# Second group's first two v products moved ahead of the first group's other five

## The chip, the cores and the metric

The kernel runs on one core of one Trainium2 chip. The metric is the device time of one execution in microseconds (us). Before the change three runs took 3236.82, 3237.32 and 3232.02 us, median 3236.82.

## The reference, cut to what matters

Two layers of a bidirectional encoder on 1024 tokens with 1024 features. The first layer mixes tokens by latent attention, the second by dilated windows in three groups; each ends with an MLP. The change touches the v part of the second layer's input projection, three products of 1024 x 1024 by 1024 x 1024, one for each group:

```python
h = rms_norm(x, norm_mix[i]) * (1 + scale1) + shift1
...
def dilated_mixer(h, pos, w_in, g_q, g_k, rel_bias, w_o):
    proj = (h @ w_in).reshape(B, S, N_DIL_GROUPS, 3, DIL_HEADS, DIL_HEAD_DIM)
    for gi, (window, dilation) in enumerate(DIL_GROUPS):
        ...
        v = proj[:, :, gi, 2]
```

shift1 and scale1, like the gates and the MLP's shift and scale, come from the conditioning vector c by `ada_w`, the modulation.

## The kernel before

Activations and weights are float32. Each matrix is split into a high part that fp32r holds (ScalarE, ACT, copies it: L121) and a low part (VectorE, DVE, subtracts: L122), and every matmul becomes three, high by high, high by low, low by high (`mm3`, L425 to L427).

`dil_v` (L1597 to L1776) computes v for each group as a 2 x 2 block product with seven multiplications in place of eight. h and the weights are cut into quarters of 512 x 512. The products of a group, by index i, are L11 R11, L12 R21, S2 T2, S1 T1, S3 T3, L22 T4 and S4 R22. The L and S sides come from h: L11 and L12 are halves for the first 512 tokens, whose high and low parts (hT) the MLP before left ready; L22 and S1 to S4 need the other 512 tokens as well. The R and T sides come from the weights: `sums` makes T1 = 12 - 11, T3 = 22 - 12, T2 = 22 - T1 and T4 = T2 - 21 in place, in the tiles (wvr) that held the quarters. Each product is 4 token tiles x 4 steps of 128 features x 3 = 48 matmuls of 128 x 128 by 128 x 512 into four PSUM banks (psv).

The loop over the 21 products (L1713 to L1774, n counts them) does for each: evict the product before (L1646), issue loads of weight quarters (L431, two DMAs of 512 KB each on the queue of SyncE, SP), make the weight sums, split the weight for the next product (`form`, wvh and wvl), split one of the h sides, and issue the 48 matmuls. Beside the first product the other 512 tokens are normalised (xh), transposed by PE (pst) and modulated (hk, half by ACT, half by DVE); beside the second their sums s1, s3 and S2, S4 are made on DVE (`h_sums`), and S2 is split (hsh, hsl). So S2 T2, the third product, is the first that needs them. Products 4 to 17 (counted from 0) also carry two `ada_step` each: one step loads 512 KB of modulation weights (adaw, L262) and adds them up on DVE (adacc: L175 the first of a vector, L176 the others).

Evictions: i = 0 copies the banks to vp by ACT; on DVE, i = 2, 3 and 4 add into vp, and i = 1, 4, 5 and 6 make vz, which POOL's queue stores. The weight tiles, the splits and vp come from one pool of 29 tiles of 4 KB a partition ("gran"); a load waits until its tile's last reader is through. A scheduler puts the instructions of each engine in order; what `pinned` marks keeps the order of the program.

Of the kernel before, what the change touches and what calls it, by code (L numbers as in the profile page):

```python
# [41 lines left out]
class K:  # L42
# [1045 lines left out]
    def mlp7(self, l, early, R, steps, xd, out, more=(), nxt=None, keep=None):  # L1088
# [16 lines left out]
        with self.tc.tile_pool(name="psM", bufs=8, space=PSUM, reuse_waits="tile") as psp:  # L1105
# [81 lines left out]
            def d_form(i, g, ld):  # L1187
                rn = order2[i][1]
                u, q = ld
                r = []  # L1190

                def split(x):
                    r.extend(self.X("d" + k, (P, 2, 512)) for k in "hl")
                    self.split(*r[-2:], x)

                split(u)
                if rn == "R11":
                    split(q["11"])
                    tt(q["12"], q["12"], q["11"], ALU.subtract)
                    kept[("T1", g)], kept[("T3", g)] = q["12"], q["11"]  # L1200
                elif rn == "T2":
                    kept[(rn, g)] = w = self.G("w2T", (P, 2, 512), F32)
                    tt(w, q["22"], kept[("T1", g)], ALU.subtract)
                    split(w)
                    tt(kept[("T3", g)], w, kept[("T3", g)], ALU.subtract)
                elif rn == "T4":
                    w = self.X("w2s", (P, 2, 512), F32)
                    tt(w, q["21"], kept[("T2", g)], ALU.subtract)
                    split(w)
                else:  # L1210
                    split(q[rn[1:]] if rn[0] == "R" else kept[(rn, g)])
                return r
# [14 lines left out]
            seq = [(c, i) for c in range(E) for i in (0, 2)]  # L1227
# [65 lines left out]
            quad = lambda n: [self.G(n, (P, 2, 512), F32) for _ in range(2)]  # L1293
            at = lambda q, t: q[t // 2][:, t % 2, :]
            xs = [None] * 8
            last = len(dsteps) - 1
            c1, c2 = slice(0, 512), slice(512, 1024)
            V, done = {}, []
# [29 lines left out]
            for n, (i, gr) in enumerate(dsteps):  # L1328
# [10 lines left out]
                if i in (3, 5) and gr < 4:  # L1339
                    t = i * 2 - 6 + gr  # L1340
                    xs[t] = self.load(xd[t * P : (t + 1) * P, :], (P, 1024), "x")
                if (i, gr) == (3, 4):
                    g = self.gate(l, 1)
# [253 lines left out]
    def dil_v(self, xs, mods, at0, keep, w11, f11, vd):  # L1597
# [5 lines left out]
        sub = lambda o, x, y: self.pinned(tt(o, x, y, ALU.subtract))  # L1603

        prod = [("L11", "R11"), ("L12", "R21"), ("S2", "T2"), ("S1", "T1"), ("S3", "T3"), ("L22", "T4"), ("S4", "R22")]
        seq = [(g, i) for g in range(3) for i in range(7)]
        hd = self.dp.tile([2, P, 2, 512], F32, name="h21")
        h0 = at0.tiles
        L = {f"L1{j + 1}": [[h0[k][2 * j + p] for k in range(2)] for p in range(2)] for j in range(2)}
        W = {(0, "11"): w11}  # L1610
        F = {0: f11}
        V = {}
        Hh, at1 = self.h_at()

        def load(g, q):
            W[(g, q)] = self.dil_w(g, q)

        def form(n):
            g, i = seq[n]
            F[n] = self.w_form(W[(g, ("11", "21", "T2", "T1", "T3", "T4", "22")[i])])  # L1620
            if i == 6:
                del W[(g, "22")]

        def sums(g, i):

            for k in range(2):
                w = lambda q: W[(g, q)][k]
                if i == 0:
                    sub(w("11"), w("12"), w("11"))
                elif i == 1:  # L1630
                    sub(w("12"), w("22"), w("12"))
                    sub(w("22"), w("22"), w("T1"))
                else:
                    sub(w("21"), w("T2"), w("21"))
            for old, new in {0: (("11", "T1"),), 1: (("12", "T3"), ("22", "T2")), 2: (("21", "T4"),)}[i]:
                W[(g, new)] = W.pop((g, old))

        quad = lambda n: [self.G(n, (P, 2, 512), F32) for _ in range(2)]
        el = lambda q, t: q[t // 2][:, t % 2, :]

        def out(g, t, c, o, ps, op=ALU.add):
            z = self.T("vz")
            tt(z, o, ps, op)
            nc.gpsimd.dma_start(out=vd[g][t * P : (t + 1) * P, c * 512 : (c + 1) * 512], in_=z)

        def evict(n, pss):  # L1646
            g, i = seq[n]
            if i in (0, 3):
                V["PQ"[i // 3]] = quad("vp")
            for t, ps in enumerate(pss):  # L1650
                p, q = (el(V[x], t) if x in V else None for x in "PQ")
                if i == 0:
                    nc.scalar.activation(p, ps, AF.Copy)
                elif i == 1:
                    out(g, t, 0, p, ps)
                elif i == 2:
                    tt(p, p, ps)
                elif i == 3:
                    tt(q, p, ps)
                elif i == 4:  # L1660
                    tt(p, p, ps)
                    out(g, t + 4, 1, q, ps)
                elif i == 5:
                    out(g, t + 4, 0, p, ps, ALU.subtract)
                else:
                    out(g, t, 1, q, ps)
            if i > 4:
                del V["PQ"[i - 5]]


        A, S = {}, {}
# [1 line left out]
        def h_form(name, src, alloc):  # L1673
            L[name] = []
            for x in src:
                f = [alloc("hs" + k, (P, 2, 512)) for k in "hl"]
                self.split(*f, x)
                L[name].append(f)
            if name == "L22":
                for k in range(2):  # L1680
                    Hh[k][2:4] = [f[k] for f in L[name]]
# [15 lines left out]
        def h_sums(k):  # L1697
            S.setdefault("S1", []).append(self.X("s1", (P, 2, 512), F32))
            S.setdefault("S3", []).append(self.X("s3", (P, 2, 512), F32))
            a11, a12, a21, a22 = keep[k], keep[2 + k], A[0][k], A[1][k]  # L1700
            tt(S["S1"][k], a21, a22)
            tt(S["S3"][k], a11, a21, ALU.subtract)
            tt(a11, S["S1"][k], a11, ALU.subtract)
            tt(a12, a12, a11, ALU.subtract)
            nc.gpsimd.dma_start(out=hd[k], in_=a21)

        with self.tc.tile_pool(name="psV", bufs=8, space=PSUM, reuse_waits="tile") as psp:
            done = None
            load(0, "21")
            load(0, "12")  # L1710
            xh = self.xhat(xs, self.X, pinv=True)
            last = len(seq) - 1
            for n, (g, i) in enumerate(seq):  # L1713
                if done:
                    evict(*done)
                if i == 0:
                    load(g, "22")
                elif i == 5:
                    load(g, "22")
                    if g < 2:  # L1720
                        load(g + 1, "11")
                elif i == 6 and g < 2:
                    load(g + 1, "21")
                    load(g + 1, "12")
                if i < 3:
                    sums(g, i)
                if n < last:
                    form(n + 1)
                if n == 1:
                    for k in range(2):  # L1730
                        h_sums(k)
                    for x, k in (("S2", 0), ("S4", 2)):
                        S[x] = keep[k : k + 2]
                    h_form("S2", S.pop("S2"), self.X)
                elif 1 < n < 6:
                    x = ("S1", "S3", "L22", "S4")[n - 2]
                    h_form(x, A.pop(1) if x == "L22" else S.pop(x), self.G if x == "L22" else self.X)
                ps = [psp.tile([P, 512], F32, tag="m", name=self.nm("psv")) for _ in range(4)]
                l, f = L[prod[i][0]], F.pop(n)
                for d in range(4):  # L1740
                    if n == 0 and d in (2, 3):
                        h_chunks(xh, 2 * d - 4, psp)
                    for t in range(4):
                        ts = slice(t * P, (t + 1) * P)
                        (lh, ll), (rh, rl) = ([x[:, d % 2] for x in y[d // 2]] for y in (l, f))
                        self.mm3(ps[t], lh[:, ts], ll[:, ts], rh, rl, d == 0, d == 3)
                done = n, ps
                if 3 < n < last - 2:
                    for _ in range(2):
                        self.ada_step(psp, "m")  # L1750
                if n == 0:
                    keep, xh = list(keep), None
                if n == last - 2:
                    raws = [self.load(hd[k], (P, 2, 512), "h21r", alloc=self.X) for k in range(2)]
                    w = self.dil_weights(0, 0, self.X)
                elif n == last - 1:
                    for raw in raws:
                        f = [self.G("hT" + k, (P, 2, 512)) for k in "hl"]
                        self.split(*f, raw)
                        for k in range(2):  # L1760
                            Hh[k].insert(len(Hh[k]) - 2, f[k])
                    raws = None
                    w = w()
            evict(*done)
        return at1, w

# [636 lines left out]
```

## Time and profile before

| | us |
|---|---|
| median of three runs (lowest, highest) | 3236.82 (3232.02, 3237.32) |
| the profiled execution's own time | 3228.74 |
| its span, first to last instruction | 3227.0 |
| busy in the span: DVE, ACT, POOL | 2383.3, 1733.2, 919.4 |
| mean granted clock of TensorE | 0.990 |
| psv matmuls, first to last start | 1421.6 to 1669.7 |
| evictions vz, vp by DVE; vp by ACT, each | 0.686, 0.687; 0.599 |

Times in rows of the profile count from the first instruction. PE is the matmul engine, PEld its weight loads. The stage of the v products is 248 us of 3227.

### The profile page before, as it was taken

The numbers are of one execution on the slowest core, as the hardware profiler recorded it, in microseconds if no ns is written. First come the engines' busy times: TensorE is split into PE (matmuls) and PEld (weight loads), VectorE is DVE, ScalarE is ACT, GpSimd is POOL, SyncE is SP. The second block draws the span as 40 slices with busy tenths as digits, with TensorE's granted clock in tenths as the row PEclk, the third lists the DMA queues.
The fourth block names the chain that finished last, engine by engine and source line by source line (L and its number), as shares of the span: only waits on it lengthen the run. The fifth ranks groups of instructions, "written<-read, shape, count | busy, mean of one in ns | idle before, by whom it ended". The sixth has DMA issues, their size and how long they took to land. (4 is left out here: it accounts for less than half of the span.)

```text
span 3227.0 us, 50801 instructions
## 1 busy us (share of the span) xinstructions
PE 3127.3 (97%) x18034; PEld 2645.7 (82%) x18034; DVE 2383.3 (74%) x4243; ACT 1733.2 (54%) x3507; POOL 919.4 (28%) x1226
## 2 busy tenths in 40 slices
PE   6999999999999999989999999999999999999999
PEld 6877677778788788877889999998998888887887
DVE  6677777746987776588757778777888588778566
ACT  5547777754554433543226677667665264444332
POOL 7464556530111100000123445444454001110010
PEclk9999999999999999999999999999999999999999
DMA  5352322253555779544638877888778536448554
GB/s 193 121 190 80 108 84 92 70 167 111 177 200 175 268 220 307 179 148 162 224 125 187 184 179 178 191 190 174 173 165 202 167 106 214 150 152 311 204 190 129
DMA packets 538926, 552.31 MB, mean 171 GB/s; under 512 B 199429, under 2 KB 421042, under 8 KB 538666
## 3 DMA queue, kind: packets, MB, share of 16 engines
q1 hardware_dynamic: 500874, 443.00, 48.4%
q0 software_dynamic: 27360, 91.31, 7.6%
q10 hardware_dynamic: 10432, 14.68, 1.6%
q8 instruction: 144, 2.36, 0.3%
q14 instruction: 116, 0.95, 0.1%
HBM read 376.17 MB, written 132.62 MB: 158 GB/s over the span
## 5 line engine op out<-in xcount | busy, mean ns | idle before, releaser
L426 PE MATMUL psm<-dl,dh 128*128 128x512 f32 x896 | 350.7, 391 | 8.3 <-DVE dl L122 8.2
L425 PE MATMUL psm<-hf,wf 128*128 128x512 f32 x896 | 350.4, 391 | 2.6 <-ACT wf L121 2.6
L426 PE MATMUL psm<-hf,wf 128*128 128x512 f32 x896 | 349.7, 390 | 0.0
L427 PE MATMUL psm<-dh,dl 128*128 128x512 f32 x896 | 349.7, 390 | 0.0
L427 PE MATMUL psm<-hf,wf 128*128 128x512 f32 x896 | 347.2, 390 | 0.4 <-DVE wf L122 0.4
L425 PE MATMUL psm<-dh,dh 128*128 128x512 f32 x896 | 335.9, 392 | 5.2 <-ACT dh L121 5.2
L425 PE MATMUL psproj<-wqkh,hTp 128*128 128x256 f32 x1024 | 302.0, 295 | 0.0
L427 PE MATMUL psproj<-wqkh,hTp 128*128 128x256 f32 x1024 | 290.4, 284 | 0.0
L426 PE MATMUL psproj<-wqkl,hTp 128*128 128x256 f32 x1024 | 290.3, 283 | 0.0
L121 ACT ACTIVATE dh<-ufr 128x1024 fp32r<-128x1024 f32 x112 | 118.3, 1056 | 175.3 <-PE psm L427 50.0
L426 PEld LDWEIGHTS psm<-dl,dh 128*128 128x128 f32 x896 | 168.7, 188 | 46.5 <-DVE dl L122 11.6
L425 PEld LDWEIGHTS psproj<-wqkh,hTp 128*128 128x128 f32 x1024 | 196.6, 192 | 8.5 <-issue 0.4
L425 PEld LDWEIGHTS psm<-dh,dh 128*128 128x128 f32 x896 | 168.5, 189 | 42.7 <-ACT dh L121 7.8
L425 PEld LDWEIGHTS psm<-hf,wf 128*128 128x128 f32 x896 | 168.7, 188 | 40.1 <-ACT wf L121 5.5
L427 PEld LDWEIGHTS psm<-hf,wf 128*128 128x128 f32 x896 | 168.5, 188 | 35.8 <-DVE wf L122 1.2
L426 PEld LDWEIGHTS psm<-hf,wf 128*128 128x128 f32 x896 | 168.7, 188 | 35.0
L427 PEld LDWEIGHTS psm<-dh,dl 128*128 128x128 f32 x896 | 168.8, 188 | 34.6
L426 PEld LDWEIGHTS psproj<-wqkl,hTp 128*128 128x128 f32 x1024 | 196.8, 192 | 0.2 <-DVE wqkl L122 0.2
L427 PEld LDWEIGHTS psproj<-wqkh,hTp 128*128 128x128 f32 x1024 | 196.4, 192 | 0.2
L122 DVE TENSOR_TENSOR dl<-ufr,dh 128x1024 fp32r<-128x1024 f32 x112 | 136.9, 1222 | 77.3 <-ACT dh L121 58.6
L756 DVE TENSOR_REDUCE mx<-pmx 128x1 f32<-128x512 f32 x256 | 165.1, 682 | 29.5 <-PE pmx L754 29.3
L122 POOL TENSOR_TENSOR pl<-p,ph 128x1024 fp32r<-128x1024 f32 x58 | 141.3, 2436 | 138.8 <-ACT ph L121 133.8
(400 smaller groups left out, 8926.4 us busy)
## 6 DMA issues: line engine op xcount, KB each, us to landing
ufr<-uf SPq DMA_DIRECT2D x112, 512.0 KB
adaw<-in_ada_w SPq DMA_DIRECT2D x96, 512.0 KB
w2r<-in_mlp_w SPq DMA_DIRECT2D x96, 512.0 KB
w1r<-in_mlp_w SPq DMA_DIRECT2D x64, 512.0 KB
bt<-bias SPq DMA_DIRECT2D x128, 256.0 KB
wqkr<-in_dil_w_in SPq DMA_DIRECT2D x96, 256.0 KB
qkv<-st SPq DMA_DIRECT2D x32, 512.0 KB
hraw<-qkv SPq DMA_DIRECT2D x32, 512.0 KB
```

What stands on the lines that cost most here:

```text
L121: nc.scalar.activation(hi, src, AF.Copy)
L122: (lo_eng or nc.vector).tensor_tensor(lo, src, hi.bitcast(F32), op=ALU.subtract)
L425: mm(out, lh, rh, start=first, stop=False)
L426: mm(out, lh, rl, start=False, stop=False)
L427: mm(out, ll, rh, start=False, stop=last)
L756: nc.vector.tensor_reduce(maxes[h][:, 2 * j + b : 2 * j + b + 1], ps, op=ALU.max, axis=AX.X)
```

## The change

The order of the 21 products becomes: the first group's first two, the second group's first two, then the first group's other five, the second group's other five, and the third group's seven. The second group's quarters 11 and 21 are loaded early for these two products, dropped, and loaded again for the sums; that is four DMAs of 512 KB more. The first group's sums and the splits of S1, S3, L22 and S4 move two products later, the second group's first sums stand beside the first group's last product. The modulation steps begin two products earlier (n = 2), and products 7 and 8, the last of the first group, have none. A group's eviction tiles are kept by group. In the MLP one condition is written twice.

```diff
@@ mlp7, d_form
                 if rn == "R11":
                     split(q["11"])
+                if rn == "R11":
                     tt(q["12"], q["12"], q["11"], ALU.subtract)
@@ dil_v
-        seq = [(g, i) for g in range(3) for i in range(7)]
+        seq = [(0, 0), (0, 1), (1, 0), (1, 1)] + [(g, i) for g in range(3) for i in range(7) if g == 2 or i > 1]
...
             if i == 6:
                 del W[(g, "22")]
+            if g == 1 and i < 2:
+                del W[(g, ("11", "21")[i])]
...
-                V["PQ"[i // 3]] = quad("vp")
+                V[g, "PQ"[i // 3]] = quad("vp")
...
-                if i == 0:
+                if n == 0:
+                    load(1, "11")
+                if (g, i) == (0, 1):
+                    load(1, "21")
+                if i == 0 and g != 1:
                     load(g, "22")
+                elif i == 4 and g == 0:
+                    load(1, "11")
+                    load(1, "12")
                 elif i == 5:
                     load(g, "22")
-                    if g < 2:
-                        load(g + 1, "11")
+                    if g == 0:
+                        load(1, "22")
+                    elif g == 1:
+                        load(2, "11")
                 elif i == 6 and g < 2:
                     load(g + 1, "21")
-                    load(g + 1, "12")
-                if i < 3:
+                    if g:
+                        load(2, "12")
+                if (g, i) == (0, 6):
+                    sums(1, 0)
+                    sums(1, 1)
+                if n in (2, 3):
+                    sums(0, n - 2)
+                elif i == 2 or i < 2 and g == 2:
                     sums(g, i)
...
-                elif 1 < n < 6:
-                    x = ("S1", "S3", "L22", "S4")[n - 2]
+                elif 3 < n < 8:
+                    x = ("S1", "S3", "L22", "S4")[n - 4]
...
-                if 3 < n < last - 2:
+                if 1 < n < last - 2 and n not in (7, 8):
                     for _ in range(2):
                         self.ada_step(psp, "m")
```

Lines behind the edits move by up to 18 (the vz and wvr sums stand at L1602 before and at L1603 after). Engine by engine, the programs hold the same rows in the same order ahead of the first product and behind the twelfth; POOL's rows are the same throughout.

The first place is PE at the start of the third product. Before, in a piece of its rows (operation, bank written <- weights moved through, h side held):

```order
L427 MATMUL psv_19266<-wvh_19115,hT_3880_18987 128x512
L425 MATMUL psv_19345<-wvh_19233,hsh_19255 128x512
L425 MATMUL psv_19346<-wvh_19233,hsh_19255 128x512
L425 MATMUL psv_19347<-wvh_19233,hsh_19255 128x512
L425 MATMUL psv_19348<-wvh_19233,hsh_19255 128x512
L426 MATMUL psv_19345<-wvl_19234,hsh_19255 128x512
L426 MATMUL psv_19346<-wvl_19234,hsh_19255 128x512
L426 MATMUL psv_19347<-wvl_19234,hsh_19255 128x512
L426 MATMUL psv_19348<-wvl_19234,hsh_19255 128x512
L425 MATMUL psv_19417<-wvh_19329,hsh_19337 128x512
```

And after the change, PE at the same place:

```order
L427 MATMUL psv_19268<-wvh_19117,hT_3880_18987 128x512
L425 MATMUL psv_19339<-wvh_19235,hT_3811_18667 128x512
L425 MATMUL psv_19340<-wvh_19235,hT_3811_18667 128x512
L425 MATMUL psv_19341<-wvh_19235,hT_3811_18667 128x512
L425 MATMUL psv_19342<-wvh_19235,hT_3811_18667 128x512
L426 MATMUL psv_19339<-wvl_19236,hT_3811_18667 128x512
L427 MATMUL psv_19339<-wvh_19235,hT_3812_18668 128x512
L426 MATMUL psv_19340<-wvl_19236,hT_3811_18667 128x512
```

The third product now reads hT, which is there since the MLP, in place of S2's hsh; four matmuls with the high part stand ahead of the first that needs the low part wvl. In each later half of a product four matmuls with wvh stand so ahead of wvl, in some places with four of the next product.

The second place is DVE ahead of that low part. Before, from the h sums to the third product's first wvl (vz evicts the second product, wvr are the weight sums):

```order
L1602 TENSOR_TENSOR s_3931_19249<-hk_18784,hk_19185 128x1024
L1602 TENSOR_TENSOR vz_19315<-vp_19223,psv_19263 128x512
L1602 TENSOR_TENSOR wvr_19105<-wvr_19105,wvr_18812 128x1024
L1602 TENSOR_TENSOR wvr_19082<-wvr_19107,wvr_19082 128x1024
L1602 TENSOR_TENSOR hk_18669<-s_3928_19241,hk_18669 128x1024
L1602 TENSOR_TENSOR hk_18784<-s_3930_19248,hk_18784 128x1024
L1602 TENSOR_TENSOR vz_19318<-vp_19223,psv_19264 128x512
L1602 TENSOR_TENSOR vz_19321<-vp_19224,psv_19265 128x512
L122 TENSOR_TENSOR wvl_19234<-wvr_19105,wvh_19233 128x1024
```

And DVE after the change, to the same product's first wvl; the modulation of the second chunk's first hk stands just ahead of this piece:

```order
L1603 TENSOR_TENSOR s_3932_19243<-hk_19149,hk_19162 128x1024
L1603 TENSOR_TENSOR s_3933_19244<-hk_18669,hk_19149 128x1024
L1698 TENSOR_SCALAR hk_19200<-pst_19207,mod_17521,mod_17903 128x512
L1603 TENSOR_TENSOR hk_18669<-s_3932_19243,hk_18669 128x1024
L1603 TENSOR_TENSOR s_3934_19250<-hk_19187,hk_19200 128x1024
L1603 TENSOR_TENSOR s_3935_19251<-hk_18784,hk_19187 128x1024
L1603 TENSOR_TENSOR hk_18893<-hk_18893,hk_18669 128x1024
L122 TENSOR_TENSOR hsl_19258<-hk_18669,hsh_19257 128x1024
L1603 TENSOR_TENSOR hk_18784<-s_3934_19250,hk_18784 128x1024
L1603 TENSOR_TENSOR vz_19317<-vp_19225,psv_19265 128x512
L1603 TENSOR_TENSOR vz_19320<-vp_19225,psv_19266 128x512
L122 TENSOR_TENSOR wvl_19236<-wvr_19105,wvh_19235 128x1024
```

The weight sums of the first group left this piece; the h sums and S2's low part stand in it ahead of wvl.

The third place is DVE in the fifth product, S2 T2 after the change, from its first low part (wvl_19408) to its second:

```order
L122 TENSOR_TENSOR wvl_19408<-wvr_19109,wvh_19407 128x1024
L1603 TENSOR_TENSOR wvr_19111<-wvr_19111,wvr_18814 128x1024
L122 TENSOR_TENSOR hsl_19578<-s_3935_19251,hsh_19577 128x1024
L1603 TENSOR_TENSOR vz_19473<-vp_19397,psv_19415 128x512
L176 SCALAR_TENSOR_TENSOR adacc_19395<-adaw_19470,cond,adacc_19395 128x1024
L1603 TENSOR_TENSOR vz_19476<-vp_19397,psv_19416 128x512
L1603 TENSOR_TENSOR vz_19479<-vp_19398,psv_19417 128x512
L1603 TENSOR_TENSOR vz_19482<-vp_19398,psv_19418 128x512
L1603 TENSOR_TENSOR wvr_19076<-wvr_19109,wvr_19076 128x1024
L1603 TENSOR_TENSOR wvr_19078<-wvr_19111,wvr_19078 128x1024
L122 TENSOR_TENSOR wvl_19412<-wvr_19111,wvh_19411 128x1024
```

Four adacc now stand on DVE ahead of wvl_19412. Before, none stood there until the low parts of the third and the fourth product were made.

More of the change, by code (lines that the diff above doesn't have):

```diff
@@ L1648, in evict @@
             if i in (0, 3):
-                V["PQ"[i // 3]] = quad("vp")
+                V[g, "PQ"[i // 3]] = quad("vp")
             for t, ps in enumerate(pss):
-                p, q = (el(V[x], t) if x in V else None for x in "PQ")
+                p, q = (el(V[g, x], t) if (g, x) in V else None for x in "PQ")
                 if i == 0:
@@ L1667, in evict @@
             if i > 4:
-                del V["PQ"[i - 5]]
+                del V[g, "PQ"[i - 5]]
         A, S = {}, {}
```

## The prediction

> **What bounds the kernel now.** I read the shares by engine first, then the stretches of this stage, then who waited for whom, then single rows. In the page's first part, each entry is an engine's busy time and instructions:
>
> ```profile
> PE 3127.3 (97%) x18034; PEld 2645.7 (82%) x18034; DVE 2383.3 (74%) x4243; ACT 1733.2 (54%) x3507; POOL 919.4 (28%) x1226
> ```
>
> TensorE (PE) is busy for 97% of the span, so only idle or slow PE time can be won. The busy times by stretch, for 60 us of the stage of the v products (start and end, length, then PE, PEld, DVE, ACT, POOL busy, granted clock, DMA share, GB/s):
>
> ```profile
> 1433.00:1445.00 12.00, 12.00 (x69) 10.44 (x68) 12.00 (x14) 3.06 (x5) 1.26 (x3) 1.00 0.38 134
> 1445.00:1457.00 12.00, 6.45 (x21) 4.13 (x20) 12.00 (x13) 10.02 (x11) 1.99 (x4) 0.75 0.38 130
> 1457.00:1469.00 12.00, 11.62 (x43) 9.06 (x41) 12.00 (x12) 4.98 (x5) 0.00 (x0) 0.82 0.00 0
> 1469.00:1481.00 12.00, 12.00 (x54) 9.95 (x53) 11.33 (x15) 3.19 (x3) 0.00 (x0) 1.00 0.20 52
> 1481.00:1493.00 12.00, 12.00 (x54) 9.95 (x53) 9.62 (x13) 2.12 (x2) 1.08 (x2) 1.00 0.76 260
> ```
>
> PE is full except from 1445 to 1469, where it also gets a granted clock of 0.75 and 0.82. DVE is full from 1433 until then: VectorE bounds this piece. The waits of PE from 1421 to 1670, the whole stage, are few:
>
> ```profile
> PE psv L425 <- ACT wvh L121: 2.4, 1, 2.4
> PE psv L425 <- ACT hsh L121: 2.0, 1, 2.0
> PE psv L426 <- DVE wvl L122: 1.5, 2, 1.2
> ```
>
> All 5.9 us lie at one place, the third product, as PE's rows in order of time show (start, length, operation, count, idle before it):
>
> ```profile
> 1435.89 0.47 PE L425 MATMUL psv<-wvh,hT 128*128 128x512 f32 x1
> ...
> 1446.67 0.39 PE L427 MATMUL psv<-wvh,hT 128*128 128x512 f32 x1
> 1449.08 1.21 PE L425 MATMUL psv<-wvh,hsh 128*128 128x512 f32 x4 [2.02 <-ACT hsh L121]
> 1451.45 2.08 PE L426 MATMUL psv<-wvl,hsh 128*128 128x512 f32 x4 [1.17 <-DVE wvl L122]
> 1455.89 2.08 PE L425 MATMUL psv<-wvh,hsh 128*128 128x512 f32 x4 [2.36 <-ACT wvh L121]
> ...
> 1464.54 0.50 PE L426 MATMUL psv<-wvl,hsh 128*128 128x512 f32 x1 [0.38 <-DVE wvl L122]
> ...
> 1469.22 0.39 PE L426 MATMUL psv<-wvl,hsh 128*128 128x512 f32 x1
> ...
> 1480.78 0.39 PE L426 MATMUL psv<-wvl,hsh 128*128 128x512 f32 x1
> ```
>
> Between the last two rows lie 51 matmuls: 11.56/51 = 0.2267 us each at full clock. The second product ends its issue at 1446.67, so the next matmul could start at 1446.9. By 1469.22 PE had issued the 48 of the third product and 4 of the fourth: 52 x 0.2267 = 11.8 us of work in 22.3 us. **10.5 us are lost here**: 5.9 idle, and 4.6 because the matmuls after the gaps run at half clock.
>
> **What the change removes.** The third and fourth products become the second group's first two, whose h sides (hT) lie ready since the first product; the S2 sums that PE waited for are now due two products, 2 x 48 x 0.2267 = 21.8 us, later. So the 10.5 us go, as far as nothing else is late. That has to be summed on DVE, whose order the change decides (rows under the change). Its steps, start to start, come from these rows:
>
> ```profile
> 1435.29 2.96 DVE L1695 TENSOR_SCALAR hk<-pst,mod,mod 128x512 f32<-128x512 f32 x4
> 1438.17 1.22 DVE L1602 TENSOR_TENSOR wvr<-wvr,wvr 128x1024 f32<-128x1024 f32 x1
> 1439.30 4.63 DVE L1602 TENSOR_TENSOR s<-hk,hk 128x1024 f32<-128x1024 f32 x4
> 1443.84 0.69 DVE L1602 TENSOR_TENSOR vz<-vp,psv 128x512 f32<-128x512 f32 x1
> 1444.44 2.36 DVE L1602 TENSOR_TENSOR wvr<-wvr,wvr 128x1024 f32<-128x1024 f32 x2
> ...
> 1468.93 0.77 DVE L175 TENSOR_SCALAR adacc<-adaw,cond 128x1024 f32<-128x1024 f32 x1
> 1469.59 1.23 DVE L122 TENSOR_TENSOR hsl<-hk,hsh 128x1024 fp32r<-128x1024 f32 x1
> ...
> 1517.10 1.28 DVE L176 SCALAR_TENSOR_TENSOR adacc<-adaw,cond,adacc 128x1024 f32<-128x1024 f32 x1
> 1518.29 1.22 DVE L1602 TENSOR_TENSOR wvr<-wvr,wvr 128x1024 f32<-128x1024 f32 x1
> ```
>
> An hk takes 2.88/4 = 0.72, a 1024-wide sum or low part (wvr, s, hk, hsl, wvl) 4.54/4 = 1.135, ending 1.23 after its start; a vz 0.60; a first adacc 0.66, a later one 1.19.
>
> **What it adds: new waits on DVE's low parts (wvl).** DVE's work is the same; only its order and PE's demands differ. The chain starts where PE has transposed the chunks:
>
> ```profile
> 1432.48 3.65 PE L320 MATMUL pst<-ident,xh 128*128 128x128 f32 x32
> ```
>
> The last 8 of 32 transposes feed the second pair of hk; the first of these can start at about 1435.7.
>
> Third product, first half: from 1435.7 two hk (1.44), eight 1024-wide (9.08) and two vz (1.20) put the start of its wvl at 1447.4, its end at 1448.65. PE starts its first four matmuls (high parts, need no wvl) at 1446.9 and is through at 1447.8: **a stall of 0.9**.
> Its second half: 1.135 + vz 0.6 + hk 1.135 + vz 0.6 + two wvr 2.27 put that wvl at 1453.2, end 1454.4. PE comes after 28 more matmuls (6.35), at 1455.0: no stall.
> Fourth product: hsl and the first adacc, which stood at 1468.93 before and now stands here, then wvr and hsl, with the wvl before them: 4 x 1.135 + 0.66 after 1453.2 is 1458.4, end 1459.6. PE: 48 matmuls after 1448.7, 1459.6: 0 to 0.1.
> Its second half ends at 1461.9, PE comes at 1465: none.
> Fifth product (S2, T2): after 1460.7 come wvl, adacc, two wvr, hsl, adacc: 4 x 1.135 + 2 x 1.19 gives 1467.6, end 1468.8. PE comes at 1459.65 + 48 x 0.2267 = 1470.5: 1.7 to spare; S2's own parts are done by 1456.
> Its second half: after 1468.7 come wvr, hsl, vz, adacc, three vz, two wvr: 4 x 1.135 + 1.19 + 4 x 0.60 = 8.1, so 1476.9, end 1478.1. PE comes 28 matmuls after 1470.5, at 1476.85: **a stall of 1.25**.
> From there DVE gets ahead, as it does in the trace after 1481. At the ninth product (R22) the wvl stands behind three vz, the third of which waits for PE's matmul three before the product's end: 0.6 + 1.23 + some 0.2 of signals - 0.68 = 1.35 after the end, where PE has four matmuls (0.9) to bridge: 0.4. At the tenth, three wvr, three vz and an adacc (3.4 + 1.8 + 1.2) stand between its two wvl, so the second ends 7.5 after the ninth product; PE is there after 32 matmuls, 7.25: 0.3.
>
> New stalls: 0.9 + 0.05 + 1.25 + 0.4 + 0.3 = **2.9 us**, if the clock stays up. Net 10.5 - 2.9 = **7.6 us gained**.
>
> **Does the clock stay up?** Idle stretches of that size elsewhere:
>
> ```profile
> 1256.77 1.19 PE L425 MATMUL psm<-dh,dh 128*128 128x512 f32 x4 [1.67 <-ACT dh L121]
> ...
> 2420.66 0.86 PE L1898 MATMUL pss<-kT 64*128 64x256 f32 x10 [1.58 <-DVE kT L1878]
> ```
>
> And the stretches behind them, with the granted clock third from the end:
>
> ```profile
> 1257.00:1259.00 2.00, 1.94 (x8) 1.28 (x8) 2.00 (x2) 0.71 (x1) 0.00 (x0) 1.00 1.06 389
> ...
> 2420.60:2422.60 2.00, 1.95 (x19) 1.81 (x20) 2.00 (x5) 0.41 (x2) 2.00 (x4) 1.00 0.00 0
> ```
>
> 1.67 and 1.58 us of idle left the granted clock at 1.00; 0.9 and 1.25, alone among full stretches, should too.
>
> The Trainium skill, page "TensorE: Matmul & The Clock Gate", section "Why this matters for your kernels", warns of idle gaps above about 3 us; by it neither the new gaps nor the old ones would cost clock, the old loss would be 5.9 instead of 10.5, and the gain 3.0. The trace differs: a gap of 2.02 followed by one of 1.17 brought the clock to 0.75.
>
> **Costed at nothing.** Four more loads of 512 KB: with a DMA share of 0.38 and 0.00 around them they are hidden; uncovered, each would hold PE for some 1.35 us (512 KB at the 389 GB/s of the stretch at 1257), 5.4 together. The second loads of the second group's quarters wait for buffers that PE frees between the fifth product and the middle of the eighth; DVE sums them in the ninth, 5 us later, and PE needs the result in the tenth. The four modulation steps moved from later to the third and fourth products are in the DVE sums above; their loads stand on SP behind the load of the second group's 21 quarter. The two products left without steps at the change of group give DVE room that no wait there needs. The evictions into a second pair of vp tiles are the same instructions. The duplicated `if` of the MLP changes no instruction. POOL's rows are the same throughout. Outside this stage every engine's rows stand in the old order, so the gain reaches the end of the chain, which is PE.
>
> **Rivals.**
> *Half clock returns.* If one of the gaps of 0.9 and 1.25 drops the clock as 2.02 did, that costs up to 4.6: gain 3.0, time 3233.8; with both, a loss of 1.6. Against it: the two rows above. For it: nothing but the nearness of 1.67 to 2.02.
> *Nothing is late.* If DVE's first hk come sooner and the waits fall into PE's bridge of four matmuls, all 10.5 are won: 3226.3.
> *Slower: DVE waits for modulation rows.* The first adacc stands on DVE ahead of the fourth product's wvl, due at 1458.3, with 0.05 to spare. Its row loads on SP behind a load that waits for PE's 26th matmul of the second product (1435.9 + 26 x 0.2267 = 1441.8). If it lands after 1455.4, all behind it on DVE, and PE, lose as much: from 7.6 us late, at 1463, there is no gain; from 14 late the kernel is slower by 0.2%, and at 20 late by 12.4: 3249.2. Against it: before, the same kind of load was issued at the same time and all transfers had ended by 1457:
>
> ```profile
> 1441.73 2.60 SPq L262 DMA_DIRECT2D adaw<-in_ada_w x2
> ```
>
> *The time doesn't follow.* Later stages lose the gain to their own waits or clock: 3236.8.
>
> **How the numbers follow.** The profiled execution took 3228.74 us (span 3227.0); less 7.6 it would take 3221.1. The runs' median is 3236.82, 8.1 above it, for a reason that the profile doesn't show; I carry that along: **3229.2 us**. Forecast (gain 5 to 9.5) 0.58; nothing late 0.12; half clock 0.20; doesn't follow 0.05; slower 0.05. The range takes in nothing late and half clock, widened below and above by the runs' own spread (3232.02 to 3237.32): 3221 to 3237. A measurement of this kernel can tell about 0.2%, 6.5 us, from no change. Faster by more: most of the forecast and the second case, 0.61; within: 0.34; slower: 0.05.
>
> **What would show it.** PE's idle 2.02, 1.17 and 2.36 gone and the clock 1.00 from 1445 to 1469; idle of about 0.9 and 1.25 before an L426 matmul of the third and fifth products, put down to wvl; the v stage, 1421 to 1670, shorter by 7.6. Wrong, if DVE idles for a DMA at the first adacc, if the clock falls in the stage, or if the stage shortens and the span doesn't.

## The result

| | before | after |
|---|---|---|
| median of 16 runs, us (lowest, highest) | 3234.81 (3228.12, 3238.13) | 3228.72 (3225.45, 3232.43) |
| after / before, 95% interval | | 0.9983 (0.9977 to 0.9990) |
| profiled execution: own time, span, us | 3228.74, 3227.0 | 3230.04, 3228.3 |
| v products, first to last start, us | 1421.60 to 1669.66: 248.06 | 1420.87 to 1663.00: 242.13 |

The changed kernel is faster by 0.17%, 5.5 us (3.2 to 7.4). That is within the 0.2% that the prediction counted as no change, and 3228.72 us is inside its range, 0.5 below its point. The gain forecast was 7.6, and 0.61 of the chance had been put on more than 0.2%; what came is the case that had 0.34. The two profiled executions do not show the gain in their spans. So the stage first.

The same five stretches of the changed kernel (start and end, length, then PE, PEld, DVE, ACT, POOL busy, granted clock, DMA share, GB/s):

```profile
1433.00:1445.00 12.00, 12.00 (x62) 10.13 (x61) 10.85 (x12) 5.03 (x7) 1.07 (x2) 1.00 0.61 193
1445.00:1457.00 12.00, 11.21 (x49) 8.94 (x49) 12.00 (x14) 5.92 (x6) 2.17 (x4) 1.00 0.80 296
1457.00:1469.00 12.00, 12.00 (x54) 9.81 (x53) 12.00 (x11) 5.25 (x7) 0.00 (x0) 1.00 0.17 52
1469.00:1481.00 12.00, 11.07 (x49) 8.81 (x48) 12.00 (x14) 5.08 (x5) 2.17 (x4) 1.00 0.47 163
1481.00:1493.00 12.00, 12.00 (x54) 9.95 (x53) 10.93 (x14) 1.75 (x2) 0.00 (x0) 1.00 0.64 219
```

PE is full or nearly so where it had 6.45 of 12, and the granted clock is 1.00 throughout. DVE is still full from 1445 to 1481: it remains the engine that PE waits for, as the waits of PE from 1421 to 1670 say (total, times, longest):

```profile
PE psv L426 <- DVE wvl L122: 2.9, 4, 0.9
```

The waits on ScalarE's hsh and wvh (2.0 and 2.4) are gone. PE's rows at the places that the prediction named, and at the first and last psv matmul:

```profile
1420.87 0.39 PE L425 MATMUL psv<-wvh,hT 128*128 128x512 f32 x1
...
1446.18 1.07 PE L425 MATMUL psv<-wvh,hT 128*128 128x512 f32 x4
1448.03 0.50 PE L426 MATMUL psv<-wvl,hT 128*128 128x512 f32 x1 [0.79 <-DVE wvl L122]
1448.37 0.39 PE L427 MATMUL psv<-wvh,hT 128*128 128x512 f32 x1
...
1474.54 1.97 PE L425 MATMUL psv<-wvh,hsh 128*128 128x512 f32 x8
1477.45 0.50 PE L426 MATMUL psv<-wvl,hsh 128*128 128x512 f32 x1 [0.93 <-DVE wvl L122]
...
1515.90 1.07 PE L425 MATMUL psv<-wvh,hsh 128*128 128x512 f32 x4
1517.30 0.50 PE L426 MATMUL psv<-wvl,hsh 128*128 128x512 f32 x1 [0.33 <-DVE wvl L122]
...
1527.43 1.07 PE L425 MATMUL psv<-wvh,hsh 128*128 128x512 f32 x4
1528.56 0.50 PE L426 MATMUL psv<-wvl,hsh 128*128 128x512 f32 x1
...
1533.69 1.52 PE L425 MATMUL psv<-wvh,hsh 128*128 128x512 f32 x6
1536.09 0.50 PE L426 MATMUL psv<-wvl,hsh 128*128 128x512 f32 x1 [0.88 <-DVE wvl L122]
...
1663.00 0.39 PE L427 MATMUL psv<-wvh,hsl 128*128 128x512 f32 x1
```

Read these by starts, since the idle figure leaves out what the pipeline bridges. The last of four starts 3 x 0.2267 after the row's start: 1446.86. The next would come at 1447.09 and comes at 1448.03, **0.94** late; and the one behind it comes 0.34 later instead of 0.23, so each restart costs 0.11 more. In the same way the five places are late by 0.94 (third product), 1.09 (fifth, second half), 0.49 (ninth), 0.22 and 1.04 (tenth, both halves): 3.78, with five restarts 4.33. The stage is shorter by 248.06 - 242.13 = **5.93 us**, so the loss before was 10.26 by this reckoning, near the 10.5 that the prediction read from the rows.

DVE's rows at two of these places: the first modulation sum, whose row might have come late, and the two low parts of the tenth product with what stands between them.

```profile
1454.76 0.76 DVE L175 TENSOR_SCALAR adacc<-adaw,cond 128x1024 f32<-128x1024 f32 x1
...
1527.29 1.22 DVE L122 TENSOR_TENSOR wvl<-wvr,wvh 128x1024 fp32r<-128x1024 f32 x1
1528.42 1.22 DVE L1603 TENSOR_TENSOR wvr<-wvr,wvr 128x1024 f32<-128x1024 f32 x1
1529.56 1.28 DVE L1603 TENSOR_TENSOR vz<-vp,psv 128x512 f32<-128x512 f32 x2
1530.75 1.28 DVE L176 SCALAR_TENSOR_TENSOR adacc<-adaw,cond,adacc 128x1024 f32<-128x1024 f32 x1
1531.95 0.68 DVE L1603 TENSOR_TENSOR vz<-vp,psv 128x512 f32<-128x512 f32 x1
1532.55 2.36 DVE L1603 TENSOR_TENSOR wvr<-wvr,wvr 128x1024 f32<-128x1024 f32 x2
1534.82 2.36 DVE L122 TENSOR_TENSOR wvl<-wvr,wvh 128x1024 fp32r<-128x1024 f32 x2
```

Neither has idle time ahead of it: DVE does not stand for the first modulation row (no bracket), and at the tenth product it simply has 7.53 us of work from one wvl's start to the next.

**Where it went in the profiled pair.** The last psv matmul before the change started at 1669.66, after it at 1663.00: 6.66 earlier, 0.73 of which were there at the first. Yet the span ends 1.3 later, so some 8 us were given back behind the stage. Two things are there. The waits of PE behind 1670 on one DMA, before and then after:

```profile
PE psav L1971 <- DMA pT<-ph: 11.1, 9, 3.3
```

```profile
PE psav L1989 <- DMA pT<-ph: 13.8, 9, 4.0
```

That is 2.7 more. And the stretches that the trace records at half clock between 1670 and 3215 sum to 23.9 us before and 34.1 after, 10.2 more, up to 5.1 us of work. An example is the gap at 2420 that kept its clock in the prediction. Before, in two stretches of the clock's own grid (next section), and after, in three:

```profile
2417.02:2420.43 3.41, 2.05 (x20) 1.68 (x19) 3.40 (x6) 2.38 (x9) 0.89 (x1) 1.00 0.59 170
2420.43:2423.84 3.41, 3.19 (x30) 3.05 (x31) 3.41 (x14) 1.22 (x4) 3.41 (x5) 1.00 0.05 10
```

```profile
2415.35:2418.76 3.41, 3.41 (x33) 3.24 (x32) 3.36 (x6) 3.41 (x13) 0.67 (x1) 1.00 0.57 152
2418.76:2422.17 3.41, 1.81 (x18) 1.48 (x19) 3.41 (x7) 0.65 (x3) 2.70 (x4) 1.00 0.27 81
2422.17:2425.58 3.41, 3.41 (x18) 3.41 (x17) 3.34 (x15) 2.94 (x14) 1.77 (x2) 0.50 0.52 108
```

The same 1.6 us of idle time lay on the border of two stretches of the grid before the change and within one after it, and only after it did it cost clock. Whether this was the change's doing or the execution's is what second profiles can tell.

### The profile page after: what moved, and what is told of

Same layout as the page of the kernel before. It is cut to its first block, busy times and chain, and to the rows that moved or that the text cites. A ratio compares the mean times of both kernels' runs of the same rounds, so it can differ in the third digit from the quotient of the medians.

```text
span 3228.3 us, 50796 instructions
## 1 busy us (share of the span) xinstructions
PE 3127.8 (97%) x18034; PEld 2646.1 (82%) x18034; DVE 2381.4 (74%) x4243; ACT 1734.1 (54%) x3507; POOL 919.3 (28%) x1226
```

## The experiments

The theory: PE lost 10 us because DVE finished the S2 sums late; the order takes this off PE's path, and what is left is DVE's backlog at the low parts wvl. Rivals: the moved modulation steps make the gain; or the clock does. "By starts" is meant as above.

**Both kernels again.** No edit.

> The kernel before, unchanged, for a second profile of it. Late-S2 theory (the 10.5 us are lost because VectorE finishes the S2 sums late): the idle before the third product's matmuls comes again at 5.5 to 6.5 us in all, and the v products take 244 to 249 us from first to last psv matmul. Clock theory (the half clock behind the gaps, and at a dozen gaps elsewhere, is not fixed: it depends on how much of a gap falls into one window of 3.41 us of a grid that starts anew in each execution): the half-clock stretch behind the third product has another length than 10.24 us or begins at another place, and gaps elsewhere that kept the clock in one profile lose it in the other; the span lies between 3226 and 3236. Rival (the clock is a fixed property of the code): the same stretches at half clock, to within 0.5 us. Ratio to before 0.9993 to 1.0007 by all.

> The changed kernel again, for a second profile. Theory of fixed waits and a clock that depends on the execution: the v products' waits repeat within 0.2 us (0.95, 1.09, 0.49, 0.23 and 1.04 by starts), no half clock between the first and the last psv matmul, 241.5 to 243 us; the stretches at half clock elsewhere differ in number or place; span 3224 to 3231, ratio to before 0.9975 to 0.9990. Rival (the first profile's later stages were slowed by the change): the same half-clock stretches behind 1900 as in its first profile, 1910, 2354 and 2422 among them.

Before again: ratio 1.0001 (0.9992 to 1.0010), v products 248.03 us; its waits of PE in the stage:

```profile
PE psv L425 <- ACT wvh L121: 2.4, 1, 2.4
PE psv L425 <- ACT hsh L121: 2.0, 1, 2.0
PE psv L426 <- DVE wvl L122: 1.7, 2, 1.3
```

After again: 0.9986 (0.9977 to 0.9995), v products 242.10 us, the five places late by 0.95, 1.08, 0.49, 0.24 and 1.05. So the 5.93 us of the stage come back to within 0.05, and the changed kernel's waits to within 0.02. The clock does not: before's second profile has a span of 3233.8, 6.9 longer, with 75.1 us at half clock in all in place of 61.4, up to 6.9 us of work; after's second profile has 23.9 us at half clock behind 1670 in place of 34.1, and none at 2422. So how much half clock a profile has belongs to the execution. Not all of the giving back does: from the last psv start to the end the changed kernel took 1565.3 and 1562.1 us, the kernel before 1557.3 and 1560.0, though in its second profile the changed kernel had no more half clock there (23.9) than the kernel before (23.9 and 27.3). PE's psav waits for pT were 13.8 and 12.6 against 11.1 and 11.3. So some of the gain may be lost again behind the stage; whether the change does that, and how, was not tested. The medians of the sixteen runs of each kernel lie 6.1 us apart.

**The order alone**, with the modulation steps where they were:

```diff
-                if 1 < n < last - 2 and n not in (7, 8):
+                if 3 < n < last - 2:
```

> The changed order of products, with the modulation steps at the fourth to seventeenth product counted from 0, as before the change, products 7 and 8 among them. Late-S2 theory: the order alone carries the gain. The third product's first half still waits 0.8 us (VectorE's rows are the same up to there); VectorE's low parts of the fifth product are due 0.4 and 0.5 late by the sum of its rows (1453.62 plus three hsl, two wvl, adacc, wvr and so on), in place of 0 and 0.93; the ninth and tenth product, with four more modulation sums of 1.19 us beside them, wait 1 to 4 us in all in place of 1.2. v products 241 to 246 us; ratio 0.9975 to 0.9995. Rival (the moved modulation steps make the gain): 0.9995 to 1.0005, v products 247 to 249.

3232.48 us, ratio 1.0003 (0.9994 to 1.0012), v products 247.68: the gain is gone, against what was expected. The third product was late by 0.94 and the fifth by 0.59 and 0.43, as expected, but the ninth by 4.96, and the gap drew 6.8 us of half clock behind it. PE's waits in the stage, then DVE's rows, then those of SP, the queue that issues the loads:

```profile
PE psv L426 <- DVE wvl L122: 6.3, 4, 4.8
```

```profile
1512.93 1.37 DVE L1603 TENSOR_TENSOR vz<-vp,psv 128x512 f32<-128x512 f32 x2 [3.65 <-PE psv L427]
1517.56 1.28 DVE L176 SCALAR_TENSOR_TENSOR adacc<-adaw,cond,adacc 128x1024 f32<-128x1024 f32 x1 [3.27 <-DMA adaw<-in_ada_w]
1518.76 0.68 DVE L1603 TENSOR_TENSOR vz<-vp,psv 128x512 f32<-128x512 f32 x1
1519.36 1.22 DVE L122 TENSOR_TENSOR wvl<-wvr,wvh 128x1024 fp32r<-128x1024 f32 x1
```

```profile
1502.16 7.50 SPq L431 DMA_DIRECT2D wvr<-in_dil_w_in  x4
1509.75 1.02 SPq L262 DMA_DIRECT2D adaw<-in_ada_w  x2
```

A modulation row (adaw) is issued at 1509.75, behind four loads of 512 KB that wait for buffers, the last until 1509.29. By the program they are quarter 22 of the first and of the second group; the four extra loads are not among them. DVE stands for 3.27 us until the row lands, with the ninth product's wvl behind it. The 0.49 of the changed kernel, these 3.27 and the sum's own 1.19 add up to 4.95, the lateness at the ninth product to within 0.01. From 1510 to 1516 the transfers run at a share of 1.03:

```profile
1510.00:1516.00 6.00, 5.83 (x26) 4.50 (x24) 1.37 (x2) 1.65 (x2) 1.08 (x2) 1.00 1.03 406
```

Whether the place in the queue or the full DMA engines make the row late was not separated. In the changed kernel products 7 and 8 have no step, and no modulation sum stands there.

**The steps alone**, in the order before:

```diff
-                if 3 < n < last - 2:
+                if 1 < n < last - 2 and n not in (7, 8):
```

> The order of products before, with the modulation steps moved as in the change (from product 2 counted from 0, none at 7 and 8). Late-S2 theory: the third product waits as before, 5.5 to 6.5 us idle, since VectorE's order up to its two low parts is the same; the four modulation sums that come two products earlier cost at most the 0.38 wait of the fourth product once more; v products 244 to 250 us, ratio 0.9993 to 1.0010. Rival (the steps make the gain): ratio 0.9977 to 0.9990, v products 241 to 243.

3231.88 us, 0.9998 (0.9989 to 1.0007), v products 246.94. The third product waits as before but for the last, on wvh, which is 1.3 shorter:

```profile
PE psv L425 <- ACT hsh L121: 2.0, 1, 2.0
PE psv L426 <- DVE wvl L122: 1.2, 1, 1.2
PE psv L425 <- ACT wvh L121: 1.1, 1, 1.1
```

The idle is 4.3 in place of 5.9, below what was expected, and the stage 1.1 shorter, too little for the runs to show. ScalarE's rows tell why. Before, the copy of that wvh (the first of the last row) stood behind four copies of other sums; with the steps moved (second piece) it is the second of three, behind two:

```profile
1450.07 2.93 ACT L121 ACTIVATE hsh<-s 128x1024 fp32r<-128x1024 f32 x3
...
1453.85 1.04 ACT L121 ACTIVATE hsh<-s 128x1024 fp32r<-128x1024 f32 x1
1454.80 2.94 ACT L121 ACTIVATE wvh<-wvr 128x1024 fp32r<-128x1024 f32 x3
```

```profile
1447.62 1.99 ACT L121 ACTIVATE hsh<-s 128x1024 fp32r<-128x1024 f32 x2
1450.12 2.95 ACT L121 ACTIVATE wvh<-wvr 128x1024 fp32r<-128x1024 f32 x3 [0.52 <-DVE wvr L1602]
```

So by these rows 1.3 of the 2.4 us put down to wvh were ScalarE's own order, not DVE's lateness. Neither part gains alone in the runs. The order opens the gain; keeping modulation sums off the change of group keeps it.

**Which of the moved steps**: steps at 4, 5, 6 and 9 to 19.

```diff
-                if 1 < n < last - 2 and n not in (7, 8):
+                if 3 < n < last and n not in (7, 8):
```

> The changed order of products, modulation steps at products 4, 5, 6 and 9 to 19 counted from 0: it keeps of the moved steps only that products 7 and 8 have none, and does not begin two products earlier. Theory (what the order needs is that no modulation sum stands at the change of group, where its row lands late): the wait of 4.96 us at the ninth product goes back to about 0.5, the fifth product's waits stay at the 0.6 and 0.4 of the order alone (same rows of VectorE up to there), the tenth's second half is not late (one modulation sum before it in place of two), in all 2.0 to 2.7 us by starts; v products 239.5 to 241.5; ratio to before 0.9970 to 0.9988. Rival (the early start at product 2 is what the order needs, to have the rows in time): the ninth product waits over 1.5, v products over 242.5, ratio 0.9985 to 1.0000.

3229.43 us, 0.9989 (0.9980 to 0.9998), v products 242.37. The ninth product was late by 0.53, as expected: leaving out products 7 and 8 is what the order needs. The tenth's second half was late by 1.61, against the expectation, and the v products stay above the 239.5 to 241.5 expected, since a modulation row is late there too and stops DVE for 0.91 us ahead of its wvl. The early start by itself brings nothing that shows (242.37 and 242.13).

**All eight hk on ScalarE**, in both kernels, and once with the steps of the run above:

```diff
-                    if j == 0:
+                    if j < 2:
```

> The changed kernel with all eight hk of the v stage modulated by ScalarE instead of four by ScalarE and four by VectorE. Late-S2 theory, by VectorE's rows: four hk of 0.72, 2.9 us, leave its chain, two of them (1.44) after PE's last transposes; the third product's wait (0.79 idle) goes, that of the fifth product's second half (0.93) goes or is under 0.2, those of the ninth and tenth (0.33 and 0.88) stay, since VectorE has caught up by then. v products 239.5 to 240.5 in place of 242.1; ratio to before 0.9965 to 0.9985, about 2 us below the changed kernel. Rival (ScalarE's eight hk, 5.6 us from 1432.1, end later than VectorE's did and hold up the sums as much): the waits at the third and fifth product stay within 0.3 us of 0.79 and 0.93, ratio 0.9975 to 0.9990.

> The kernel before with all eight hk on ScalarE. Late-S2 theory (the third product waits for VectorE's chain of hk, weight sums and S2 sums; that two of its waits are put down to ScalarE is only because ScalarE's copies come last in that chain): 1.44 to 2.9 us leave the chain, the idle of 5.9 becomes 3.0 to 4.5, v products 242 to 246.5, ratio 0.9980 to 0.9997. Rival (ScalarE itself is late): its hk now end later, the idle stays at 5.5 or more, v products 247.5 to 250, ratio 0.9995 to 1.0010.

> The same steps as the run above, and all eight hk on ScalarE. Late-VectorE theory: the third product does not wait, the fifth's second half (0.65 with the steps of the change) stands behind one modulation sum less and does not wait, the tenth's second half neither; only the ninth's 0.5 stays. v products 238.0 to 239.5, ratio to before 0.9955 to 0.9978. Rival (a modulation row lands late elsewhere and stops VectorE): a wait over 1 us remains, v products over 240.5, ratio 0.9970 to 0.9990.

In the changed kernel: 3225.65 us, 0.9978 (0.9968 to 0.9988), v products 240.76; the third product no longer waits, the fifth's second half is late by 0.65, where less than 0.2 was expected, the ninth and tenth as before. In the kernel before: 3228.92 us, 0.9986 (0.9977 to 0.9995), v products 245.93, 2.1 less, half clock for 6.8 us in place of 10.2; its idle time fell less than expected, to 5.0. With 2.7 us of work more, ScalarE made PE wait less, so the waits put down to its hsh and wvh were at least in part DVE's lateness passed on. By the runs alone this one edit of the old kernel can't be told from the whole change (0.9986 here, 0.9983 and 0.9986 there); the stage tells them apart, 2.1 us against 5.9. In the changed kernel with the steps of the run above: 3226.39 us, 0.9981 (0.9972 to 0.9990), v products 240.30, above the 239.5 expected at most; the third and fifth product do not wait, but the tenth's second half is late by 1.65, again behind a modulation row that comes 0.98 late, as the rival had it.

**The steps off the tenth product too**: hk on ScalarE, steps at 3 to 6 and 10 to 19.

```diff
-                if 1 < n < last - 2 and n not in (7, 8):
+                if 2 < n < last and n not in (7, 8, 9):
```

> The changed order, all eight hk on ScalarE, modulation steps at products 3 to 6 and 10 to 19 counted from 0. Late-VectorE theory: no modulation sum stands before the tenth product's second half, so its wait (1.05 with the steps of the change, 1.65 where a row landed late) goes; the ninth's 0.5 stays, the fifth's second half waits up to 0.65. v products 238.5 to 240.0, ratio to before 0.9955 to 0.9978. Rival (another row lands late): a wait over 1 us remains, v products over 240.3.

3224.89 us, **0.9974 (0.9964 to 0.9985)**, v products 239.19, as expected: the lowest median here, though its interval meets that of hk on ScalarE alone. PE's waits in the stage:

```profile
PE psv L426 <- DVE wvl L122: 0.8, 2, 0.5
```

**A wider gap at the third product**, twice the same kernel and once wider. The sums go into a tile that nobody reads; the result stays what it was.

```diff
+                if n == 1:
+                    z = self.T("vz")
+                    for _ in range(2):
+                        self.pinned(tt(z, el(V[0, "P"], 0), el(V[0, "P"], 1)))
                 if n < last:
                     form(n + 1)
```

> The changed kernel with two more VectorE sums of 128x512 (0.60 each, into a tile that nobody reads) ahead of the third product's first low part. Late-VectorE theory: its idle time grows from 0.79 by 1.2 to 2.0, and what stands behind it on VectorE and PE moves along. Clock by windows: the clock is set for each stretch of 3.41 us of a grid by how much of the stretch before was busy, and halves below about half; so 2.0 us of idle halves it for 3.41 us, at a price of 1.7 us, where 1.7 or more of them fall into one stretch (about 6 phases in 10), and costs nothing beside itself otherwise; the grid of this execution, read from its other half-clock stretches, says which. Rival (a single gap below 3 us never costs clock): clock 1.00 behind it at any phase. Rival (a gap of 2.0 always does, as before the change): half clock at any phase. v products 243.2 to 245.2.

> The same kernel as gap2_a again, in another execution, so at another place of the grid: the same idle time of 2.0 to within 0.1, and the clock behind it by the same rule of its own grid; it may differ from gap2_a.

> Three such sums, and by VectorE's rows one more vz ahead of the low part: 4 x 0.60 = 2.4, so idle of 3.2 in place of 0.79. By windows 1.7 or more fall into one stretch of 3.41 at nearly every phase: half clock for 3.41 us behind it, v products 242.1 + 2.4 + 1.7, 245 to 247. Rival (only gaps over 3 us after full work cost clock): half clock too, so it does not tell these two apart; it bounds the price of one us of VectorE here, 1 us of PE.

The gap grew to 2.58 in both executions, not the 2.0 expected (a third vz of 0.60 had moved ahead as well), and to 3.19 with three sums. The stretches of each execution's grid around it, of gap2_a and of gap2_b:

```profile
1444.71:1448.12 3.41, 2.99 (x14) 2.14 (x12) 3.41 (x5) 1.85 (x2) 0.00 (x0) 1.00 1.04 423
1448.12:1451.53 3.41, 1.24 (x5) 1.05 (x6) 3.41 (x5) 1.54 (x3) 2.04 (x4) 1.00 1.03 410
1451.53:1454.95 3.42, 3.42 (x9) 2.65 (x8) 3.42 (x4) 1.69 (x2) 0.14 (x1) 0.50 0.66 267
```

```profile
1445.91:1449.33 3.42, 2.44 (x11) 1.69 (x9) 3.42 (x5) 2.12 (x2) 0.49 (x1) 1.00 1.02 419
1449.33:1452.74 3.41, 1.81 (x8) 1.50 (x9) 3.41 (x5) 1.83 (x2) 1.69 (x4) 1.00 1.03 414
1452.74:1456.15 3.41, 3.41 (x17) 2.81 (x16) 3.41 (x4) 1.13 (x2) 0.00 (x0) 1.00 0.51 204
```

The same gap of the same kernel halved the clock in one execution, where 2.17 us of it lay in one stretch, and not in the other, where 0.98 and 1.60 lay in two. Both rivals of this run fall. The v products took 244.25 and 243.37: the half clock cost 0.9, not 1.7, since at full clock (gap2_b) PE was late by 0.45 at the fourth product and by 0.12 more at the tenth, and the slower PE of gap2_a was not. In both the fifth product's wait of 1.09 is gone, as DVE has caught up while PE came later. The wider gap gave one half-clock stretch and 244.93, just under the expected 245 to 247; there too the fifth product no longer waits.

## The prediction, point by point

- **The loss of 10.5 us at the third product, and its cause**: right in the main. 10.26 by the two stages, and the same in a second pair. That DVE's chain counts is shown from both sides: hk taken off DVE shortened the old stage by 2.1 us, and 1.8 us put on DVE widened the new gap by 1.79. But 1.3 of the 5.9 idle came from ScalarE's own order at the wvh copy (the steps alone), which the prediction did not see.
- **Third product, stall of 0.9**: 0.94. **Fourth**: none, right. **Fifth, first half 1.7 to spare, second half 1.25 late**: none, and 1.09. **Ninth, 0.4**: 0.49.
- **Tenth, second half 0.3**: the step that was most off in size. It was late by 1.04, and its first half by 0.22. The rows between the two wvl were counted rightly, but the sum of 7.5 to the second one's end has room for one low part of 1.135, not two: it takes the first as done when the ninth product ends. The first only started then, at 1527.29, so 7.53 later the second one starts, and it ends 1.1 after that.
- **Restarts**: not priced. 0.11 at each of five places, 0.55.
- The sum: 10.5 - 2.9 = 7.6 forecast, 10.26 - 4.33 = 5.93 measured. Of the 1.67 between them the tenth makes 0.96, the restarts 0.55, the third, fourth, fifth and ninth together -0.08, and 0.24 is the difference between the two reckonings of the old loss, not assigned to a place.
- **The point, 3229.2, against 3228.72**: two errors met. The gain was too large by 1.7, and the base, the median of three runs, 3236.82, was 2.0 above that of sixteen. That the point came within 0.5 is luck.
- **"The two products left without steps at the change of group give DVE room that no wait there needs"**: wrong. With steps there PE is 4.96 us late at the ninth product, and the whole gain is gone (1.0003). The mechanism is that of the rival on the slower side, a modulation row that lands late ahead of a wvl; it was weighed at the first modulation sum, where DVE did not wait for a DMA, and not at the change of group, where four other loads of 512 KB stand ahead of the row and wait for buffers. For the four extra loads themselves nothing did show: PE has no wait in the stage that is put down to a load.
- **The clock stays up**: right for these gaps (1.00 in all stretches of both profiles), but by a reason that was too simple, the length of the gap. What counts is how much of it falls into one stretch of 3.41 us. A gap of 0.8 to 1.1 alone among full stretches leaves each of them busy for two thirds or more, and above 55% hardly any was followed by half clock (last section). The gap of 1.6, within one stretch busy for 53%, had no such margin.
- **The gain reaches the end**: on average, for the most part (5.5 and 4.5 us by the two ratios, 5.9 in the stage; the intervals also allow all of it). In the single profiled pair it doesn't show. The 8.1 us between the profiled execution and the median, which the prediction carried along unexplained, may be of the same kind: the second profile of the same kernel was 6.9 longer, with up to 6.9 us of work lost to half clock.

## What to carry to other kernels

Where work is put earlier to fill a gap, ask of everything it displaces, at the place where it now stands, which load it waits for and what that load is queued behind: here the order gained nothing until the modulation steps were taken off the place where the loads of two groups' quarters stand ahead of their rows. A wait put down to one engine may be another's lateness passed on, or that engine's own order, or some of each; taking work off the engine that is full, even onto the one that is named, tells. And one profiled pair can hide a gain of this size: compare the stage that was changed, start to start, and leave the total to many runs.

## What the hardware showed that was not expected

The granted clock goes in stretches of 3.41 us on a grid that lies elsewhere in each execution; every half-clock stretch recorded is one or several of them, but for the last, which the end cuts off. Over the 14 profiles, behind the first 60 us, I summed PE's busy time in each stretch of full clock: of 120 that were busy for less than 45%, 119 were followed by half clock; of 82 between 45% and 55%, 45 were; of 12510 above 55%, 8 were, unexplained. So a gap costs clock by how it lies on the grid, not by its length alone. The Trainium skill, page "TensorE: Matmul & The Clock Gate", section "Why this matters for your kernels", warns of idle gaps above about 3 us. The runs differ: gaps of 1.6 and 2.58 us each halved the clock in one execution and left it in another. That the spread of one kernel's runs (3228 to 3238 before) comes from this grid fits the two profiles of it, but was not tested further.
